# Two-layer expert model with a two-half second block: the memory's keys projected before each cross attention instead of in front of the experts

## The chip, the core and the metric

One core of a Trainium2 chip (trn2) runs the whole program. The metric is the device time of one execution in microseconds; the kernel before took 2755.97 us, the median of three runs.

The engines are TensorE (PE: matmuls and transposes; its weight loads, PEld, overlap them), VectorE (DVE), ScalarE (ACT), GpSimd (POOL) and SyncE (SP), which issues nearly all DMA transfers. Each engine runs its own queue strictly in order and waits on semaphores for the others.

## The reference, cut to what matters

512 tokens of width 1024, all float32. The first block has two layers of a mixer and 32 experts each. The second block has two halves: self attention, cross attention to a memory of 256 tokens, and a gated feed-forward, each with a norm before and a norm behind. Memory keys and values depend on nothing but the input `mem` and weights:

```python
def hier_moe(x, w_group, b_group, w_expert, b_expert, w1, w3, w2):
    ...
    def expert_block(args):
        rows, rw, e = args
        xi = x_pad[rows]
        h = jax.nn.silu(xi @ w1[e]) * (xi @ w3[e])
        return (h @ w2[e]) * rw[:, None]
    ...
def memory_cross_attention(u, mem_n, wq, wkv, wo):
    q = split_heads(u @ wq, X_HEADS)
    k, v = jnp.split(mem_n @ wkv, 2, axis=-1)
    k = split_heads(k, X_HEADS)
    v = split_heads(v, X_HEADS)
    s = jnp.einsum('bhqd,bhkd->bhqk', q, k,
                   preferred_element_type=jnp.float32) * (X_HEAD_DIM ** -0.5)
    p = jax.nn.softmax(s, axis=-1)
    o = jnp.einsum('bhqk,bhkd->bhqd', p.astype(v.dtype), v)
    return merge_heads(o) @ wo

    ...

        u = rms_norm_2(h, mem_pre_g[i])
        y = memory_cross_attention(u, rms_norm_2(mem, mem_kv_g[i]), x_wq[i], x_wkv[i], x_wo[i])
        h = h + rms_norm_2(y, mem_post_g[i])
```

## The kernel before

**Numbers.** A product of float32 matrices is made of three matmuls (`mm3`): each operand is split into a high part and a remainder (`wh`, `wl` for weights, `xth`, `xtl` for activations), and hi·hi, hi·lo and lo·hi are added in PSUM. ACT writes the high part, DVE the remainder (`split`, `wload`). For a projection the weights are loaded as tiles `raw` of [128, 1024], 512 KB, from a heap of 46 such tiles that all stages share. The experts' matmuls take the raw float32 tiles.

**Order.** The program writes its operations down in one order (`run`, L2299 on); a list scheduler (`flush`) then deals them to the engines. It keeps, per engine, a window of operations in the order in which they were written, and picks by a cost model (`price`, L215) when each is free and ready. The order that comes out is fixed: every engine runs its queue as written. All recorded instructions carry line L385.

**Stages.** Per layer of the first block: mixer (`f1`), router (`route`), then, before the change, `mem_kv(l)` (L1002) for half `l` of the second block, then the experts (`moe`). The router's DVE chain ends in slot lists (`slg`), permutation tiles (`P`) and token indices for GpSimd's gathers (`xg`), from which PE makes `xe`; each pair of experts then runs up (`mm<-raw,xe`), down (`mm<-raw,t`) and a combine. A loop for overflowing slots ahead of the experts is a barrier of all engines. Expert weights are `raw<-w` on SP's queue, 192 loads per layer.

`mem_kv(i)` loads the memory (two tiles `mem`), norms it (`xn<-mem`), transposes it (16 transposes, `tp<-const,xn`), projects the keys (8 chunks × 8 × 3 = 192 matmuls of 256 columns, `mm<-xth,wh 128x256` and its two fellows, out to `memk` in DRAM) and the values (96 matmuls of 512 columns, out to `memv`).

Each half of the second block is `longnet` or `diff` (self attention with its output projection), `cross` (L1033) and `ffn`. The tail of the output projection (`tail_post`, L722) works per tile of 128 tokens: adds the last partial sum (`y<-y,mm`), makes the norm's factor `n_r`, adds to `x` in two halves (`x<-y,n_r,x`, `x<-t,n_r,x`), and hands the tile to the chain (`chain`, L748), which transposes it (eight `tp<-const,x` per tile, 32 in all) and splits the result (`xtl<-tp,xth`). `cross` then projects q with `x_wq`: the first half of its columns in two token halves (192 matmuls of 256 columns), the rest in 96 of 512. It reads the keys back (`kraw`, split to `kh`, `kl`) and the values (`vraw`); its first score matmul is `mm<-kh,xth`.

```python
def to_T(s, t, xn, xT, pairs=None):
    ...
    for q in range(2) if pairs is None else ():
        tp = s.TP()
        for i in range(4):
            nc.tensor.transpose(tp[:, i * 128:(i + 1) * 128], ...)
```

Of the kernel before, what the change touches and what calls it, by code (L numbers as in the profile page):

```python
# [10 lines left out]
F32 = mybir.dt.float32  # L11
# [9 lines left out]
DSIZE = {F32: 4, F32R: 4, I32: 4, U32: 4, BF16: 2}  # L21
EPS = 1e-6
D = 1024
# [62 lines left out]
class Recorder:  # L86
# [127 lines left out]
    @staticmethod  # L214
    def price(eng, method, outs, ins, k):  # L215

        def free(x):
            n = 1
            for v in x.shape[1:]:
                n *= int(v)  # L220
            return n
        if eng == "ALL":
            return 2500, 0
        n = max(free(x) for x in outs + ins) if method != "matmul" else free(outs[0])
        if eng == "PE":
            dt = ins[-1].dtype if method == "matmul" else ins[0].dtype
            f = (2 if method == "transpose" else 4) if dt == F32 else 1
            if method == "matmul" and dt == F32 and outs[0].shape[0] == 64:

                f = 2  # L230
            return n * f * 0.417, None
        psum = any(x.tensor.space == PSUM for x in ins)
        if eng == "SP" or "dma" in method:
            b = outs[0] if outs[0].tensor.space != bass.MemoryType.DRAM else ins[0]
            return (1040, 4500 if "indirect" in method else 1710) if eng == "POOL" else (475, 1100), int(b.shape[0]) * free(b) * DSIZE[b.dtype] / 360
        small = sum(isinstance(x, bass.AP) for x in (k.get("scale"), k.get("bias"), k.get("accum_out")))
        if eng == "ACT":
            return (51 if psum else 93) + n * 0.833 + 93 * small, None
        if eng == "POOL":
            if k.get("op") == ALU.pow:  # L240
                return 300 + 165 * n, None
            return 150 + n * (1 if method == "memset" else 2.1), None
        fast = method in ("tensor_scalar", "tensor_copy", "memset") and not psum
        return 69 + n * (0.52 if fast else 1.04) + 61 * sum(free(x) == 1 for x in ins), None
# [230 lines left out]
class Kern:  # L475
# [102 lines left out]

    def wload(s, W, k0, nk, c0, ncol, gain=None, lo_eng="V"):

        nc = s.nc
        per = min(1024 // ncol, 4)
        res = []
        eng = lo_eng
        for a in range(0, nk, per):
            q = min(per, nk - a)
            raw, hi, lo = s.H(name="raw"), s.H(F32R, "wh"), s.H(F32R, "wl")
            nc.sync.dma_start(raw[:, :q * ncol].rearrange("p (j c) -> p j c", j=q),
                              W[(k0 + a) * 128:(k0 + a + q) * 128, c0:c0 + ncol].rearrange("(j p) c -> p j c", p=128))
            if gain is None:  # L590
                s.split(raw[:, :q * ncol], hi[:, :q * ncol], lo[:, :q * ncol])
            for i in range(q):
                v = slice(i * ncol, (i + 1) * ncol)
                if gain is not None:
                    s.split_gain(raw[:, v], hi[:, v], lo[:, v], gain[:, k0 + a + i:k0 + a + i + 1], eng[(a + i) % len(eng)])
                res.append((hi[:, v], lo[:, v]))
        return res
# [34 lines left out]

    def out_proj(s, actT, nk, W, resident, tail, k0=0, accum=None, post=None, gain=None):

# [4 lines left out]
        for a in range(0, nk, 4):  # L639
            m = min(4, nk - a)  # L640
            w = s.wload(W, k0 + a, m, 0, 512, gain)
            for t in range(NT):
# [23 lines left out]
        for a in range(0, nfree, 4):  # L666
            m = min(4, nfree - a)
            w = s.wload(W, k0 + a, m, 512, 512, gain)
            for t in range(NT):
                for i in range(m):  # L670
                    k = a + i
                    s.mm3(pss[t], actT.get(k, t * 128, t * 128 + 128), w[i],
                          k == 0, k == nk - 1)
        w = s.wload(W, k0 + nfree, resident, 512, 512, gain)
        for t in range(NT):
# [323 lines left out]
        return ys  # L999


    def mem_kv(s, i):  # L1002

        nc = s.nc
        W = s.I["x_wkv_2"][i]
        kd = s.dr.tile([D, 256], F32, name=f"memk{i}")
        vd = s.dr.tile([256, D], F32, name=f"memv{i}")
        g = s.gain(s.I["mem_kv_g_2"][i])
        mT = s.newXT(256)
        for t in range(2):  # L1010
            m = s.H(name="mem")
            nc.sync.dma_start(m, s.I["mem_2"][0, t * 128:(t + 1) * 128, :])
            xn = s.norm(m, g)
            s.to_T(t, xn, mT)
        for cb in range(2):
            def ck(c, ps):
                o = s.T2()
                nc.scalar.copy(o[:, 0:256], ps[:, 0:256])
                r = (cb * 4 + c) * 128
                nc.sync.dma_start(kd[r:r + 128, :], o[:, 0:256])  # L1020
            s.lin_T(mT, 8, W, cb * 512, 128, 4, ck)
        for cb in range(2):
            w = s.wload(W, 0, 8, D + cb * 512, 512)
            for t in range(2):
                ps = s.PS()
                for k in range(8):
                    s.mm3(ps, mT.get(k, t * 128, t * 128 + 128), w[k], k == 0, k == 7)
                o = s.T2()
                nc.scalar.copy(o, ps)
                nc.sync.dma_start(vd[t * 128:(t + 1) * 128, cb * 512:(cb + 1) * 512], o)  # L1030
        return kd, vd

    def cross(s, i, act, kv, nxt):  # L1033
        nc = s.nc
# [1266 lines left out]
    def run(s):  # L2301
        I = s.I
        s.setup()
        c = s.chain(I["attn_norm"][0])
        c.prep()
        for t in range(NT):
            c(t)
        kv = []
        for l in range(2):
            s.f1(l, c.act, s.chain_route(l), I["x"][0] if l == 0 else s.xd)  # L2310
            s.route()
            kv.append(s.mem_kv(l))
            raws = [s.pair_raw(l, p) for p in range(2)]
            c = s.chain(I["attn_norm"][1] if l == 0 else I["mix_pre_g_2"][0], s.spill)
            s.moe(l, raws, c)
        for i in range(2):
            n = s.chain(I["mem_pre_g_2"][i])
            (s.longnet, s.diff)[i](c.act, n, s.xd)
            c = s.chain(I["ffn_pre_g_2"][i])
            s.cross(i, n.act, kv[i], c)  # L2320
            n = s.chain(I["mix_pre_g_2"][1], s.spill) if i == 0 else s.store
            s.ffn(i, c.act, n)
            c = n
        s.nc.flush()
# [16 lines left out]
```

## Time and profile before

| | |
|---|---|
| median of 3 runs | 2755.97 us (2755.9 to 2762.24) |
| the profiled execution's own time | 2757.27 us |
| its span | 2755.5 us |
| mean granted clock of TensorE | 0.991 |
| PE busy | 2671.8 us, 97% |
| DVE, ACT, POOL busy | 1521.8, 1167.3, 637.5 us |
| DMA | 421.92 MB, mean 153 GB/s |

The profile is one execution seen by the hardware profiler. It was read in this order: the page's busy times; windows, which give busy time, granted clock (1.00 is 2.4 GHz) and DMA rate of a stretch; waits, which sum an engine's idle time by what ended it; and the timeline, which lists single instructions with their start, duration and the idle time before them. In the timeline `mm<-xth,wh 128*128 128x256` is a matmul with stationary `xth` and moving `wh` into a PSUM tile `mm` of 128 × 256. A matmul's duration includes the time until its result is there, so the price of one in a row of many is the distance between their starts.

### The profile page before, as it was taken

What the parts mean: (1) busy time and instruction counts of PE and PEld (TensorE: products, weight loads), DVE (VectorE), ACT (ScalarE), POOL (GpSimd) and SP (SyncE); (2) the same over time, 40 slices, a digit from 0 to 9 for tenths busy, and PEclk for the clock granted to TensorE, in tenths of its full rate; (3) what the DMA queues carried; (4) which work ended last, traced back from release to release, by engine and by line L of the source; (5) the groups of instructions that cost most, each with busy time, mean ns of one, the idle gap of its engine ahead of it and who ended that gap; (6) DMA issues with size and microseconds to landing.
All of it is one profiled execution on the core that took longest, in us unless ns stands there. A gap on an engine that the chain in (4) does not pass through costs nothing.

```text
span 2755.5 us, 40546 instructions
## 1 busy us (share of the span) xinstructions
PE 2671.8 (97%) x15112; PEld 2143.7 (78%) x15112; DVE 1521.8 (55%) x3259; ACT 1167.3 (42%) x2390; POOL 637.5 (23%) x754
## 2 busy tenths in 40 slices
PE   8999999999999999999999999999999999999998
PEld 7878765568888665568788988888888879888887
DVE  6696544355787443353698553344548885543433
ACT  5555212144455111154696452233447765432331
POOL 2623101004332100013364111001325541110012
PEclk9999999999999999999999999999999999999999
DMA  6125999961136999930113322333411133322321
GB/s 178 30 78 174 333 408 406 375 209 42 40 125 227 370 408 398 355 106 24 53 56 138 115 77 73 94 101 107 132 39 62 62 124 105 94 73 84 112 94 44
DMA packets 224056, 421.92 MB, mean 153 GB/s; under 512 B 46064, under 2 KB 112368, under 8 KB 223856
## 3 DMA queue, kind: packets, MB, share of 16 engines
q1 hardware_dynamic: 219248, 410.89, 42.7%
q0 software_dynamic: 4608, 8.40, 0.8%
q8 instruction: 121, 1.98, 0.3%
q14 instruction: 79, 0.65, 0.1%
HBM read 410.83 MB, written 16.78 MB: 155 GB/s over the span
## 4 chain that ended last, share of the span: by engine, by line
PE 58%; DVE 5%; ACT 2%; POOL 1%; issue 1%; DMA 0%; DVEq 0%; ACTq 0%; POOLq 0%
PE mm L385 54%; PE tp L385 3%; DVE wl L385 1%; DVE x L385 1%; DVE t L385 1%; ACT t L385 0%; DVE nm L385 0%; ACT qh L385 0%; DVE pt L385 0%; ACT pring L385 0%; POOL ra L385 0%; POOL t L385 0%; DVE y L385 0%; DMA raw<-x_wq 0%; DVE xnm L385 0%
## 5 line engine op out<-in xcount | busy, mean ns | idle before, releaser
L385 PE MATMUL mm<-wh,xth 128*128 128x512 f32 (+3 forms) x1088 | 404.9, 397 | 1.3 <-DVE xtl L385 0.7
L385 PE MATMUL mm<-wl,xth 128*128 128x512 f32 (+3 forms) x1088 | 402.9, 394 | 1.4 <-DVE wl L385 1.4
L385 PE MATMUL mm<-wh,xtl 128*128 128x512 f32 (+3 forms) x1088 | 402.2, 393 | 0.2 <-DVE xtl L385 0.2
L385 DVE SCALAR_TENSOR_TENSOR wl<-raw,pre_g,wh 128x512 fp32r<-128x512 f32 (+4 forms) x400 | 284.7, 752 | 150.2 <-ACT wh L385 120.2
L385 PE MATMUL mm<-xth,wh 128*128 128x512 f32 (+1 forms) x1184 | 365.6, 359 | 0.8 <-ACT xth L385 0.3
L385 PE MATMUL mm<-xth,wl 128*128 128x512 f32 (+1 forms) x1184 | 364.5, 358 | 0.0
L385 PE MATMUL mm<-xtl,wh 128*128 128x512 f32 (+1 forms) x1184 | 362.8, 357 | 1.5 <-DVE xtl L385 1.5
L385 ACT ACTIVATE wh<-raw,pre_g 128x512 fp32r<-128x512 f32 (+4 forms) x400 | 252.0, 686 | 68.8 <-DMA raw<-w_gate_up 49.1
L385 PEld LDWEIGHTS mm<-xtl,wh 128*128 128x128 f32 x1184 | 219.2, 190 | 32.8 <-DVE xtl L385 1.7
L385 PEld LDWEIGHTS mm<-xth,wh 128*128 128x128 f32 x1184 | 219.3, 190 | 32.3 <-ACT xth L385 0.8
L385 PEld LDWEIGHTS mm<-xth,wl 128*128 128x128 f32 x1184 | 219.4, 190 | 30.8
L385 PE MATMUL mm<-raw,xe 128*64 128x256 f32 x2048 | 234.3, 383 | 3.0 <-issue 3.0
L385 PEld LDWEIGHTS mm<-wh,xth 128*128 128x128 f32 x1088 | 204.9, 189 | 35.5 <-ACT xth L385 2.2
L385 PEld LDWEIGHTS mm<-wl,xth 128*128 128x128 f32 x1088 | 205.0, 189 | 35.2 <-DVE wl L385 2.3
L385 PEld LDWEIGHTS mm<-wh,xtl 128*128 128x128 f32 x1088 | 205.3, 189 | 33.1 <-DVE xtl L385 0.6
L385 PEld LDWEIGHTS mm<-raw,xe 128*64 128x64 f32 x2048 | 144.3, 137 | 85.1 <-issue 12.8
L385 POOL TENSOR_TENSOR ffl<-t,ffh 128x512 fp32r<-128x512 f32 x44 | 60.0, 1365 | 543.6 <-ACT ffh L385 505.7
L385 DVE TENSOR_TENSOR wl<-raw,wh 128x1024 fp32r<-128x1024 f32 x112 | 144.4, 1294 | 51.6 <-ACT wh L385 43.7
L385 ACT ACTIVATE t<-mm 128x256 f32<-128x256 f32 (+3 forms) x72 | 28.8, 403 | 290.3 <-PE mm L385 230.3
L385 ACT CAST wh<-raw 128x1024 fp32r<-128x1024 f32 (+2 forms) x128 | 120.1, 956 | 34.7 <-DMA raw<-w_down 29.7
L385 PE MATMUL mm<-raw,t 128*64 128x512 f32 x512 | 126.8, 641 | 7.5 <-ACT t L385 7.4
L385 PE MATMUL mm<-wh,ffh 128*128 128x512 f32 x352 | 130.1, 389 | 0.0
(338 smaller groups left out, 4911.3 us busy)
## 6 DMA issues: line engine op xcount, KB each, us to landing
raw<-w SPq DMA_DIRECT2D x384, 512.0 KB
raw<-w_gate_up SPq DMA_DIRECT2D x176, 256.0 KB
raw<-w_down SPq DMA_DIRECT2D x40, 512.0 KB
raw<-x_wkv SPq DMA_DIRECT2D x32, 512.0 KB
raw<-a_w_in SPq DMA_DIRECT2D x24, 512.0 KB
raw<-b_w_in SPq DMA_DIRECT2D x24, 512.0 KB
raw<-w_in SPq DMA_DIRECT2D x24, 384.0 KB
raw<-w_out SPq DMA_DIRECT2D x16, 512.0 KB
```

The lines of the kernel that those rows point to most:

```text
L385: r = o.fn(*o.a, **o.k)
```

## The change

`mem_kv` is cut in three. `mem_T` holds the norm and transposes of the memory, `mem_keys` is `mem_T` with the projection of the keys, `mem_values` is `mem_T` with that of the values. `mem_values` stays in front of the experts. `mem_keys` is called after the self attention of the half and before `cross`. Norm and transposes of the memory are thus done twice per half. `price` also reckons a DMA of long runs at 400 bytes per ns instead of 360, for the scheduler only.

```diff
@@ -230,9 +230,19 @@
                 f = 2
             return n * f * 0.417, None
         psum = any(x.tensor.space == PSUM for x in ins)
+
+        def s_rate(aps):
+
+            x = next(v for v in aps if v.tensor.space == bass.MemoryType.DRAM)
+            n = 1
+            for st, c in reversed(list(x.ap)):
+                if st != n and c > 1:
+                    break
+                n *= c
+            return 400 if n * 4 >= 4096 else 360
         if eng == "SP" or "dma" in method:
             b = outs[0] if outs[0].tensor.space != bass.MemoryType.DRAM else ins[0]
-            return (1040, 4500 if "indirect" in method else 1710) if eng == "POOL" else (475, 1100), int(b.shape[0]) * free(b) * DSIZE[b.dtype] / 360
+            return (1040, 4500 if "indirect" in method else 1710) if eng == "POOL" else (475, 1100), int(b.shape[0]) * free(b) * DSIZE[b.dtype] / s_rate(outs + ins)
         small = sum(isinstance(x, bass.AP) for x in (k.get("scale"), k.get("bias"), k.get("accum_out")))
         if eng == "ACT":
             return (51 if psum else 93) + n * 0.833 + 93 * small, None
@@ -999,26 +1009,36 @@
         return ys
 
 
-    def mem_kv(s, i):
-
-        nc = s.nc
-        W = s.I["x_wkv_2"][i]
-        kd = s.dr.tile([D, 256], F32, name=f"memk{i}")
-        vd = s.dr.tile([256, D], F32, name=f"memv{i}")
+    def mem_T(s, i):
+
         g = s.gain(s.I["mem_kv_g_2"][i])
         mT = s.newXT(256)
         for t in range(2):
             m = s.H(name="mem")
-            nc.sync.dma_start(m, s.I["mem_2"][0, t * 128:(t + 1) * 128, :])
+            s.nc.sync.dma_start(m, s.I["mem_2"][0, t * 128:(t + 1) * 128, :])
             xn = s.norm(m, g)
             s.to_T(t, xn, mT)
+        return mT
+
+    def mem_keys(s, i, kd):
+
+        nc = s.nc
+        W = s.I["x_wkv_2"][i]
+        mT = s.mem_T(i)
+        yield
         for cb in range(2):
             def ck(c, ps):
                 o = s.T2()
                 nc.scalar.copy(o[:, 0:256], ps[:, 0:256])
                 r = (cb * 4 + c) * 128
                 nc.sync.dma_start(kd[r:r + 128, :], o[:, 0:256])
-            s.lin_T(mT, 8, W, cb * 512, 128, 4, ck)
+            yield from s.lin_T_steps(mT, 8, W, cb * 512, 128, 4, ck)
+
+    def mem_values(s, i, vd):
+
+        nc = s.nc
+        W = s.I["x_wkv_2"][i]
+        mT = s.mem_T(i)
         for cb in range(2):
             w = s.wload(W, 0, 8, D + cb * 512, 512)
             for t in range(2):
@@ -1028,7 +1048,6 @@
                 o = s.T2()
                 nc.scalar.copy(o, ps)
                 nc.sync.dma_start(vd[t * 128:(t + 1) * 128, cb * 512:(cb + 1) * 512], o)
-        return kd, vd
 
     def cross(s, i, act, kv, nxt):
         nc = s.nc
@@ -2309,7 +2328,8 @@
         for l in range(2):
             s.f1(l, c.act, s.chain_route(l), I["x"][0] if l == 0 else s.xd)
             s.route()
-            kv.append(s.mem_kv(l))
+            kv.append((s.dr.tile([D, 256], F32, name=f"memk{l}"), s.dr.tile([256, D], F32, name=f"memv{l}")))
+            s.mem_values(l, kv[l][1])
             raws = [s.pair_raw(l, p) for p in range(2)]
             c = s.chain(I["attn_norm"][1] if l == 0 else I["mix_pre_g_2"][0], s.spill)
             s.moe(l, raws, c)
@@ -2317,6 +2337,7 @@
             n = s.chain(I["mem_pre_g_2"][i])
             (s.longnet, s.diff)[i](c.act, n, s.xd)
             c = s.chain(I["ffn_pre_g_2"][i])
+            s.merge(s.mem_keys(i, kv[i][0]))
             s.cross(i, n.act, kv[i], c)
             n = s.chain(I["mix_pre_g_2"][1], s.spill) if i == 0 else s.store
             s.ffn(i, c.act, n)
```

**PE at the first junction from self attention to cross attention.** `tp<-const,x` are the transposes of x, `mm<-wh,xth 128x512` and its fellows belong to the output projection of the self attention, `mm<-xth,wh 128x256` before the change to q; of before:

```order
L385 MATMUL tp<-const,x 128x128 x4
L385 MATMUL mm<-wh,xth 128x512
L385 MATMUL mm<-wl,xth 128x512
L385 MATMUL mm<-wh,xtl 128x512
L385 MATMUL mm<-xth,wh 128x256
L385 MATMUL mm<-xtl,wh 128x256
L385 MATMUL mm<-xth,wl 128x256
...
L385 MATMUL mm<-xth,wl 128x256
L385 MATMUL tp<-const,x 128x128 x4
L385 MATMUL mm<-xth,wh 128x256
L385 MATMUL mm<-xtl,wh 128x256
L385 MATMUL tp<-const,x 128x128 x4
```

and of the change, where `tp<-const,xn` are the transposes of the memory and the `128x256` matmuls are the keys:

```order
L395 MATMUL mm<-wh,xth 128x512
L395 MATMUL mm<-wl,xth 128x512
L395 MATMUL mm<-wh,xtl 128x512
L395 MATMUL tp<-const,x 128x128 x20
L395 MATMUL tp<-const,xn 128x128 x8
L395 MATMUL tp<-const,x 128x128 x4
L395 MATMUL tp<-const,xn 128x128 x8
L395 MATMUL mm<-xth,wh 128x256 x5
L395 MATMUL mm<-xtl,wh 128x256
L395 MATMUL mm<-xth,wl 128x256
L395 MATMUL mm<-xth,wh 128x256
```

The transposes of the last two tiles stood inside q; now those of all tiles but the first stand together with the memory's, ahead of the keys, and q stands behind the keys. The second half has the same pattern.

**DVE at the same junction**, of before, from the x of the last two tiles to the last split of the chain:

```order
L385 SCALAR_TENSOR_TENSOR x<-y,n_r,x 128x512
L385 SCALAR_TENSOR_TENSOR x<-t_3049,n_r,x 128x512
L385 SCALAR_TENSOR_TENSOR x<-y,n_r,x 128x512
L385 SCALAR_TENSOR_TENSOR x<-t_3057,n_r,x 128x512
L385 TENSOR_TENSOR vl<-vraw,vh 128x1024
L385 TENSOR_TENSOR xtl<-tp,xth 128x2x128 x7
L385 TENSOR_SCALAR pre_v<-nss 128x1 x2
L385 TENSOR_TENSOR xtl<-tp,xth 128x2x128
L385 TENSOR_TENSOR vl<-vraw,vh 128x1024
```

and of the change, where `xn<-mem` is the memory's norm and `wl<-raw,wh 128x1024` a split of the keys' weights:

```order
L395 TENSOR_TENSOR wl<-raw,wh 128x1024
L395 TENSOR_SCALAR n_r<-nss 128x1
L395 SCALAR_TENSOR_TENSOR x<-y,n_r,x 128x512
L395 TENSOR_TENSOR xtl<-tp,xth 128x2x128
L395 SCALAR_TENSOR_TENSOR xn<-mem,n_r,gain 128x1024
L395 TENSOR_SCALAR n_r<-nss 128x1
L395 TENSOR_TENSOR xtl<-tp,xth 128x2x128 x2
L395 SCALAR_TENSOR_TENSOR x<-t_2977,n_r,x 128x512
L395 SCALAR_TENSOR_TENSOR xn<-mem,n_r,gain 128x1024
L395 TENSOR_TENSOR xtl<-tp,xth 128x4x128
...
L395 TENSOR_SCALAR pre_v<-nss 128x1
L395 SCALAR_TENSOR_TENSOR wl<-raw,pre_g,wh 128x512 x8
```

The splits of q's weights (`wl<-raw,pre_g,wh`), which stood ahead of the chain, and those of keys and values (`kl`, `vl`) stand behind it now; the memory's norm and splits stand in it.

**SP in front of the first experts**, of before (`raw<-w` are expert weights):

```order
L385 DMA raw<-x_wkv 128x2x512 x6
L385 DMA xm_590<-xn 128x1024
L385 DMA raw<-x_wkv 128x2x512 x5
L385 DMA xm_590<-xn 128x1024
L385 DMA memk_665<-t_697 128x256
L385 DMA raw<-w 128x1024
L385 DMA pre_g<-attn_norm 128x8x1
L385 DMA raw<-w 128x1024 x3
L385 DMA memk_665<-t_699 128x256
L385 DMA raw<-w 128x1024 x9
L385 DMA memk_665<-t_701 128x256
```

and of the change:

```order
L395 DMA raw<-x_wkv 128x2x512 x3
L395 DMA xm_590<-xn 128x1024
L395 DMA raw<-x_wkv 128x2x512 x2
L395 DMA xm_590<-xn 128x1024
L395 DMA raw<-x_wkv 128x2x512 x3
L395 DMA raw<-w 128x1024
L395 DMA pre_g<-attn_norm 128x8x1
L395 DMA raw<-w 128x1024 x6
L395 DMA xm_590<-xn 128x1024
L395 DMA raw<-w 128x1024 x5
L395 DMA xm_590<-xn 128x1024
```

Eight loads of `x_wkv` and the stores of the keys no longer stand among and ahead of the expert weights.

## Rows read from the trace of the kernel before

**Rows 1.** The page: busy time of each engine, its share of the span, instructions.

```profile
PE 2671.8 (97%) x15112; PEld 2143.7 (78%) x15112; DVE 1521.8 (55%) x3259; ACT 1167.3 (42%) x2390; POOL 637.5 (23%) x754
```

**Rows 2.** Windows (start:end, length, busy us by engine, PE's granted clock, DMA share, GB/s): front, junction.

```profile
core 0: us, PE busy (x) PEld busy (x) DVE busy (x) ACT busy (x) POOL busy (x), PEclk, DMA share, GB/s
...
280.00:330.00 50.00, 50.00 (x383) 44.86 (x383) 33.26 (x138) 10.05 (x19) 7.42 (x7) 1.00 0.97 357
...
1490.00:1495.00 5.00, 4.88 (x17) 3.96 (x17) 3.15 (x9) 2.40 (x7) 0.55 (x1) 0.54 0.00 0
```

**Rows 3.** PE's waits, first expert stage (280 to 560): total us, times, longest.

```profile
PE tp L385 <- DVE t L385: 4.9, 4, 1.6
...
PE tp L385 <- DMA raw<-w: 1.4, 1, 1.4
```

**Rows 4.** Window 350 to 500; SP's waits from 340 to 400, and from 460 to 520.

```profile
350.00:500.00 150.00, 145.93 (x1014) 89.72 (x1014) 63.00 (x126) 26.39 (x49) 9.91 (x10) 1.00 1.03 407
...
SPq L385 <- DMA raw<-w: 41.3, 43, 2.4
...
SPq L385 <- PE mm L385: 31.2, 21, 4.6
```

**Rows 5.** Timeline of PE, first junction: start us, us, instruction [idle before <-releaser].

```profile
1488.61 1.08 PE L385 MATMUL tp<-const,x 128*128 128x128 f32 x4 [3.37 <-issue]
...
1496.85 0.27 PE L385 MATMUL mm<-xth,wh 128*128 128x256 f32 x1
...
1505.58 0.60 PE L385 MATMUL tp<-const,x 128*128 128x128 f32 x4
...
1542.28 0.28 PE L385 MATMUL mm<-kh,xth 128*128 128x256 f32 x1
```

**Rows 6.** Timeline of DVE, first junction.

```profile
1484.89 1.02 DVE L385 TENSOR_TENSOR n_r<-ss 128x1 f32<-128x1 f32 x1 [0.19 <-ACT t L385]
...
1486.77 1.74 DVE L385 SCALAR_TENSOR_TENSOR x<-y,n_r,x 128x512 f32<-128x512 f32 x1
...
1491.11 0.75 DVE L385 SCALAR_TENSOR_TENSOR x<-y,n_r,x 128x512 f32<-128x512 f32 x1 [0.67 <-POOL n_r L385]
...
1495.39 0.42 DVE L385 TENSOR_TENSOR xtl<-tp,xth 128x256 fp32r<-128x256 f32 x1 [1.54 <-ACT xth L385]
...
1502.30 0.75 DVE L385 SCALAR_TENSOR_TENSOR x<-y,n_r,x 128x512 f32<-128x512 f32 x1
```

**Rows 7.** Timelines of DVE (first line) and PE, second junction.

```profile
2252.26 1.24 DVE L385 TENSOR_TENSOR n_r<-ss 128x1 f32<-128x1 f32 x1
...
2261.99 0.74 PE L385 MATMUL mm<-xth,wh 128*128 128x256 f32 x4
...
2308.40 0.28 PE L385 MATMUL mm<-kh,xth 128*128 128x256 f32 x1
```

**Rows 8.** Timeline of PE, first front: keys, first expert matmul.

```profile
279.52 0.40 PE L385 MATMUL mm<-xtl,wh 128*128 128x256 f32 x2
...
279.99 0.40 PE L385 MATMUL mm<-xth,wh 128*128 128x256 f32 x2
...
328.42 3.67 PE L385 MATMUL mm<-raw,xe 128*64 128x256 f32 x32
```

**Rows 9.** Timeline of DVE, first routing chain.

```profile
282.90 1.21 DVE L385 TENSOR_TENSOR wl<-raw,wh 128x1024 fp32r<-128x1024 f32 x1
...
298.47 0.29 DVE L385 TENSOR_TENSOR t<-t,tp 128x128 f32<-128x128 f32 x1 [3.26 <-PE tp L385]
...
300.61 0.24 DVE L385 TENSOR_SCALAR slg<-rt_sl 128x8 f32<-128x8 f32 x2
...
310.64 3.71 DVE L385 TENSOR_SCALAR P<-const,slg 128x512 bf16<-128x512 f32 x8 [3.87 <-PE mm L385]
```

**Rows 10.** Timeline of SP's queue, first front: the first load of expert weights.

```profile
282.30 0.42 SPq L385 DMA_DIRECT2D raw<-w  x1
```

**Rows 11.** Timeline of DVE: norm of a memory tile.

```profile
261.93 1.27 DVE L385 SCALAR_TENSOR_TENSOR xn<-mem,n_r,gain 128x1024 f32<-128x1024 f32 x1
```

## Prediction

> **What bounds the kernel now.** I read the page first, then windows of the stages that the change touches, then the waits in them, and last single instructions. TensorE (PE) is busy for 2671.8 us [rows 1] of a span of 2755.5, so only some 84 us are not matmul work. The time is PE's work plus the few places where PE stands uncovered: moving a piece of PE work gains only if it covers more where it goes than where it was.
>
> The **front of the first experts** is PE's. PE is busy in all 50 us from 280 to 330 [rows 2], with the keys, the values and the routing sums. In the whole expert stage PE's largest wait is 4.9 us for a tile that DVE writes; it waits 1.4 us for expert weights [rows 3]. The DMA engines are full there (share 1.03, 407 GB/s), but SP, which issues the loads, waits first for earlier loads (41.3 of 60 us) and later for PE to free tiles (31.2 of 60) [rows 4]: loads run ahead, and PE sets the pace.
>
> The **junction** from the self attention to the cross attention is a chain on DVE: a tile's last norm, x, transposes, splits. In the first half PE stands 3.37 us before the first transposes at 1488.61, then runs the projection's left-over matmuls, and takes up the q projection at 1496.85 [rows 5], while x of the last tiles is only made at 1502.30 [rows 6] and their last transposes stand inside q, at 1505.58 [rows 5]. So q covers the second part of the chain. In the second half the chain begins at 2252.26 and q at 2261.99 [rows 7].
>
> **The change part by part.** *Keys leave the front.* Per half 192 matmuls of 256 columns go. Four of them take 0.47 us (279.52 to 279.99) [rows 8], so 0.12 each and 23.0 us. By PE alone the first expert matmul would come at 328.42 − 23.0 = 305.4. It also needs the routing chain: slg at 300.61, P at 310.64 for 3.71 us [rows 9], then sums, gather and transposes until 328.42, 14.1 us after P. Eight weight splits wl (spacing 1.15) leave that chain, 9.2 us, a wait of 3.26 us for a transpose on PE shrinks by an unknown part [rows 9], and P now follows slg at once. So slg comes at 291.4 with that wait or 288.1 without, P ends 3.7 later, and the first expert matmul stands at 309.2 or 305.9. The front gains 19 to 22.5 us; I take 21, between its two ends, and the same for the second layer, which is built alike: −42.
>
> Eight of the 16 loads of x_wkv also leave SP's queue, 512 KB each. A load takes about 1.3 us in the full stretch (512 KB at 407 GB/s [rows 4]), so expert weights begin some 10 to 16 us before 282.30 [rows 10], where PE wants them 21 earlier. The lead of the loads over PE is 328.42 − 282.30 = 46 us today and would be 35 to 41. With 1.4 us of waits on loads today I cost that at nothing; if the lead were too short, it is the third rival. The barrier of the overflow loop moves ahead of the first expert matmul; every engine pays it once either way, nothing. The planner's new DMA rate leaves the order elsewhere nearly as it was: nothing.
>
> *Keys come to the junction*, +23.0 us of PE per half. In PE's new order all 32 transposes of x and all 16 of the memory stand ahead of the first key matmul, and q behind the keys. So keys start only when the DVE chain ends, and q covers none of it. DVE's work, in the new order from the first n_r to the memory's second xn: n_r 1.0; three tail sums, 1.8; eight halves of x, two at 1.7 (beside GpSimd) and six at 0.67; three wl, 3.4; two xn, 2.4; pairs and singles of xtl (0.34 each), about 4; small ones, 0.9 [rows 6, 9, 11]. That is 20.9 us, and the last eight transposes with ACT's cast behind it 1.5. DVE's waits in this stretch are now 0.67 and 1.54 [rows 6] and shorter ones, 2.6 in all. So keys start 25 us after the first n_r. The ends are 20 (norms of the memory slip into DVE's waits) and 28 (tail sums wait behind the ten left-over matmuls at the lower clock).
>
> Then come keys, 23.0, and q. From 1496.85 to the first score matmul (kh) at 1542.28 are 45.4 us; less some 1.4 for the 16 transposes inside, q takes 44.0 [rows 5]. The first score matmul now comes 25 + 23.0 + 44.0 = 92.0 us after the first n_r, where today it is 1542.28 − 1484.89 = 57.4 [rows 5, 6] and 2308.40 − 2252.26 = 56.1 [rows 7]: +34.6 and +35.9. Of these 70.5 us, 46.0 are the keys and 24.5 is the lost cover of q, the repeated norm of the memory and its transposes within it.
>
> *Loads at the junction.* Two memory tiles, a gain and 8 x_wkv loads are added; SP passes them ahead of x_wq, half of which now waits for tiles that the keys free. The DMA share in this stretch is 0.00 [rows 2], and 23 us of keys lie over it: nothing; without that cover four loads, 5 us.
>
> *Clock.* After the wait of 3.37 us the granted clock reads 0.54 from 1490 to 1495 [rows 2, 5], about 1.2 GHz, so those 5 us lose 2.3. The new wait is longer and broken by transposes; the first keys may run at the lower level too, 0 to 3 us per half. I take nothing, since the loss of today is in the 57.4, and keep 3 for the range. The Trainium skill ("TensorE: Matmul & The Clock Gate", section "What's actually happening") says that the throttled state is the default and activity releases it. By that rule, which speaks against the change, both halves begin their keys at 1.2 GHz and the sum would be some 5 us higher; the first junction's row agrees with the rule.
>
> **Sum:** −42 + 70.5 = +28.5 us. The profiled execution took 2757.27 us, 1.3 above the median of 2755.97, so 2785.8 in its terms and 2784.5 in those of the median. I predict **2784 us**, 1% slower. A measurement of this kernel can tell 0.3%, 8.3 us, from no change.
>
> **The rivals.** *First, faster: keys before x.* The keys need nothing of x. If PE began them at the first n_r, they would fill the 3.37 us, the chain would run under them, and q would follow whole: 23.0 + 15 left-over matmuls (3.4) + 48 transposes (4.5) + 44.0 = 75 us, +17.5 and +18.8. With −42 that is −6; with the front at its best (−23 each) −10, so 2746 to 2750. For it: memory and its weights can lie ready early. Against it: PE's new queue, with 48 transposes ahead. It decides for faster only if keys start within a few us of the first n_r. Chance 0.08.
>
> *Second, no change: a short chain.* q's 15 splits no longer lie ahead of the chain, nor kl and vl in it (four operations like wl, 4.6 us). If keys start after 14 us, the junctions cost 23.6 + 24.9 = 48.5, the sum is +6.5 and the time 2762. For it: some of the chain is waiting, which another order may fill. Against it: wl, xn and the memory's xtl take the place of what goes. Chance 0.14.
>
> *Third, much slower: loads set the experts' pace.* Then a half gains in front only its 8 loads, 10.4 us, and the sum is 70.5 − 20.8 = +50: 2806. For it: DMA share 1.03. Against it: PE's 1.4 us. Chance 0.10. [...]
>
> **How the numbers follow.** The forecast has 0.68. Its own range, with the chain at 20 to 28 us, the clock and the front's ends, is 2771 to 2798. The range to hold 8 in 10 is **2758 to 2802**: it takes in the second rival and leaves out the first and the third. Faster 0.09, same 0.13, slower 0.78.
>
> **What would show it.** Right: no keys in the first front and its expert matmuls 19 to 22.5 us earlier; at both junctions PE idle for some 10 to 13 us more, among transposes, first key matmul 20 to 28 us after the first n_r, then 23 us of keys and 44 of q; PE's busy time up by a few us. Wrong: keys among the projection's left-over matmuls; a front that hardly moves; or PE waiting for expert weights far longer than 1.4 us.

## The result and the profile after

The changed kernel takes **2781.55 us** (median of four runs, 2779.26 to 2787.06) against 2757.41 for the kernel before in the same comparison: ratio 1.0083, 95% interval 1.007 to 1.0097. That is 24.1 us slower, where 28.5 were forecast (2784 us, range 2758 to 2802). The profiled execution took 2787.06 us with a span of 2785.3, at the upper end of the runs, so its stages sum to some 6 us more than the medians differ.

The page's line of busy times, which answers to [rows 1]:

```profile
PE 2687.9 (97%) x15144; PEld 2163.5 (78%) x15144; DVE 1523.7 (55%) x3275; ACT 1176.6 (42%) x2406; POOL 642.4 (23%) x758
```

PE's busy time grew by 16 us for 32 more transposes (some 4 us). Eight transposes are busy for 1.97 us at a granted clock of 0.50 and for 1.08 us as it comes back (both below), so a stretch of lower clock shows in the busy time too.

To see where the time went, I cut the timeline of PE at the same instructions in each trace: the first transposes of x that feed the router, the first and the last up matmul of a layer's experts (start to start), the first transposes of x at a junction, the first score matmul. Times between them in us:

| stretch | before | change | move alone | rate alone | rate 440 | move, 440 |
|---|---|---|---|---|---|---|
| start to first layer's router | 245.1 | 254.2 | 247.2 | 255.1 | 245.9 | 246.6 |
| router to first expert matmul, layer 1 | 83.3 | 70.2 | 71.4 | 85.8 | 89.8 | 74.4 |
| first to last expert up matmul, layer 1 | 262.7 | 250.1 | 264.0 | 250.9 | 236.7 | 237.8 |
| router to first expert matmul, layer 2 | 86.1 | 68.5 | 67.4 | 85.2 | 87.7 | 71.8 |
| first to last expert up matmul, layer 2 | 260.1 | 249.9 | 261.5 | 250.0 | 237.8 | 235.8 |
| first junction, to the first score matmul | 53.7 | 87.9 | 87.4 | 53.2 | 53.1 | 87.5 |
| second junction | 52.1 | 88.0 | 88.0 | 52.1 | 52.2 | 87.9 |
| all the rest | 1712.4 | 1716.5 | 1711.4 | 1711.7 | 1709.4 | 1707.5 |

The last four columns are experiments, below. The up matmuls of the first layer, before and with the change, as the view of the tile `xe` lists them (durations in ns, then the first and the last start):

```profile
L385 PE MATMUL mm<-raw,xe x1024: 379/379/687, 328.4 to 591.1; 128*64 128x256 f32 x171
L395 PE MATMUL mm<-raw,xe x1024: 379/379/687, 324.4 to 574.5; 128*64 128x256 f32 x171
```

From before to the change, the junctions cost 34.2 + 35.9 = 70.1 us, the fronts give back 13.1 + 17.6 = 30.7, the expert stages give back 12.6 + 10.2 = 22.8, and the first layer's mixer takes 9.1 more: +25.7, with the rest +29.8. Of the rest's 4.1 us, 3.7 are in the second layer's mixer (240.8 for 237.1 us, at a mean granted clock of 0.97 for 0.99). The forecast had the junctions right, and missed the others with errors that nearly cancel.

The expectations recorded below give smaller values for the expert stages (256.2 and 253.4 us before, 244.2 and 243.7 with the rate alone, 247.7 and 241.1 with the rate for expert weights only). Those end at the start of a row that merges many matmuls, up to 7 us ahead of the last one; a range given for a stage there is best read as a difference from these values.

**The junction.** PE's timeline of the change, first junction, start us, us, instruction [idle before <-releaser], answers to [rows 5]:

```profile
1454.62 1.32 PE L395 MATMUL tp<-const,x 128*128 128x128 f32 x8 [1.09 <-DVE x L395]
1460.42 1.97 PE L395 MATMUL tp<-const,x 128*128 128x128 f32 x8 [4.49 <-DVE x L395]
1464.18 1.12 PE L395 MATMUL tp<-const,x 128*128 128x128 f32 x4 [1.79 <-DVE x L395]
1465.80 1.94 PE L395 MATMUL tp<-const,xn 128*128 128x128 f32 x8 [0.50 <-DVE n_r L395]
1467.53 1.04 PE L395 MATMUL tp<-const,x 128*128 128x128 f32 x4
1468.39 1.08 PE L395 MATMUL tp<-const,xn 128*128 128x128 f32 x8
1470.51 1.11 PE L395 MATMUL mm<-xth,wh 128*128 128x256 f32 x5 [1.05 <-ACT xth L395]
...
1537.61 0.28 PE L395 MATMUL mm<-kh,xth 128*128 128x256 f32 x1
```

Each of the waits shown before transposes of x ends with x on DVE. Nothing lies between the waits but transposes, and the keys start at 1470.51. DVE in the same stretch, answering to [rows 6]:

```profile
1444.43 0.38 DVE L395 TENSOR_TENSOR n_r<-ss 128x1 f32<-128x1 f32 x1 [0.85 <-ACT t L395]
...
1464.38 1.27 DVE L395 SCALAR_TENSOR_TENSOR xn<-mem,n_r,gain 128x1024 f32<-128x1024 f32 x1
...
1466.96 1.27 DVE L395 SCALAR_TENSOR_TENSOR xn<-mem,n_r,gain 128x1024 f32<-128x1024 f32 x1
```

From the first n_r at 1444.43 to the first key are 26.1 us, and to the first score matmul 93.2; the forecast had 25 and 92.0. In the second half (first line DVE, the others PE), answering to [rows 7], they are 25.0 and 92.1:

```profile
2246.23 0.52 DVE L395 TENSOR_TENSOR n_r<-ss 128x1 f32<-128x1 f32 x1 [0.87 <-ACT t L395]
...
2271.21 1.11 PE L395 MATMUL mm<-xth,wh 128*128 128x256 f32 x5 [0.35 <-ACT xth L395]
...
2338.30 0.28 PE L395 MATMUL mm<-kh,xth 128*128 128x256 f32 x1
```

The windows of the first junction, columns as in [rows 2]:

```profile
1455.00:1460.00 5.00, 0.93 (x7) 0.45 (x5) 5.00 (x13) 4.47 (x12) 3.27 (x3) 0.82 0.35 121
1460.00:1465.00 5.00, 2.79 (x12) 2.29 (x12) 4.11 (x10) 4.09 (x10) 2.62 (x3) 0.50 0.00 0
1465.00:1470.00 5.00, 3.96 (x22) 3.29 (x20) 5.00 (x10) 5.00 (x12) 0.55 (x1) 0.66 0.00 0
1470.00:1475.00 5.00, 4.49 (x35) 4.30 (x36) 5.00 (x12) 2.72 (x6) 1.54 (x2) 1.00 0.01 3
```

DVE is busy almost throughout, PE is not. The granted clock is 0.50 (1.2 GHz) while PE waits and transposes, and 1.00 from the first keys on, so the transposes paid for the lower clock and the keys did not.

**The front of the experts.** Windows of the change, columns as in [rows 2]:

```profile
280.00:310.00 30.00, 30.00 (x190) 24.47 (x188) 27.19 (x132) 6.43 (x13) 8.99 (x7) 1.00 1.03 408
310.00:330.00 20.00, 9.99 (x80) 6.75 (x78) 4.30 (x15) 1.17 (x2) 2.22 (x2) 0.66 0.79 270
```

PE is full until 310 and then half idle. Its waits from 260 to 560 (total, times, longest us), answering to [rows 3]:

```profile
PE tp L395 <- issue: 10.0, 1, 10.0
PE tp L395 <- DVE t L395: 3.0, 2, 1.5
PE mm L395 <- ACT t L395: 1.4, 3, 0.5
```

One wait of 10.0 us stands at the barrier of the overflow loop. The kernel before waits 3.0 us there, at 338.00, behind its first expert matmuls; that row belongs to the list of [rows 3], where it is the longest single wait. In the second layer the barrier takes 8.2 us against 2.0. The rows, before in the first layer, then the change and before in the second:

```profile
PE mm L385 <- issue: 3.0, 1, 3.0
...
PE tp L395 <- issue: 8.2, 1, 8.2
...
PE tp L385 <- issue: 2.0, 1, 2.0
```

Behind the barrier PE's clock is down, and the first expert matmuls take 5.59 us where they took 3.67 [rows 8] (first line DVE, then PE):

```profile
298.66 3.26 DVE L395 TENSOR_SCALAR P<-const,slg 128x512 bf16<-128x512 f32 x8
...
320.51 0.19 PE L395 MATMUL tp<-rt_rec,P 128*128 128x6 bf16 x1 [9.99 <-issue]
...
324.45 5.59 PE L395 MATMUL mm<-raw,xe 128*64 128x256 f32 x32
```

P stands 44.4 us behind the router's first transposes (298.66 and 254.24), where it stood 65.6 behind them in [rows 9]: 21 us earlier, as forecast. But from P's end to the first expert matmul 22.5 us pass, where the forecast kept the 14.1 of before. That stretch holds the barrier, and there the front loses 8.4 us of its gain. No wait on expert weights is left among PE's waits: the loads were early enough, with their first issue at 271.72 instead of 282.30 [rows 10].

### The profile page after: what moved, and what is told of

Its sections match the earlier page's. It is cut to its first block, busy times and chain, and to the rows that moved or that the text cites. A ratio compares the mean times of both kernels' runs of the same rounds, so it can differ in the third digit from the quotient of the medians.

```text
span 2785.3 us, 40687 instructions
## 1 busy us (share of the span) xinstructions
PE 2687.9 (97%) x15144; PEld 2163.5 (78%) x15144; DVE 1523.7 (55%) x3275; ACT 1176.6 (42%) x2406; POOL 642.4 (23%) x758
## 4 chain that ended last, share of the span: by engine, by line
PE 82%; DVE 9%; ACT 3%; POOL 2%; issue 2%; DMA 1%; SPq 0%; DVEq 0%; ACTq 0%; POOLq 0%
PE mm L395 75%; PE tp L395 7%; DVE wl L395 2%; DVE t L395 2%; DVE x L395 1%; DMA raw<-w 1%; ACT t L395 1%; DVE qkm L395 1%; POOL t L395 1%; ACT wh L395 0%; ACT qh L395 0%; SPq L395 0%; DVE nm L395 0%; DVE pt L395 0%; POOL ra L395 0%
## 5 line engine op out<-in xcount | busy, mean ns | idle before, releaser
L395 ACT ACTIVATE wh<-raw,pre_g 128x512 fp32r<-128x512 f32 (+4 forms) x400 | 252.7, 686 | 70.2 <-DMA raw<-w_gate_up 48.7
L395 PEld LDWEIGHTS mm<-xtl,wh 128*128 128x128 f32 x1184 | 219.1, 189 | 30.7
L395 ACT CAST wh<-raw 128x1024 fp32r<-128x1024 f32 (+1 forms) x128 | 120.8, 955 | 37.0 <-DMA raw<-w_down 30.2
L395 ACT ACTIVATE t<-mm 128x256 f32<-128x256 f32 (+3 forms) x72 | 28.7, 402 | 243.9 <-PE mm L395 153.6
L395 PE MATMUL mm<-wh,ffl 128*128 128x512 f32 x352 | 129.1, 390 | 0.0
```

The lines of the kernel that those rows point to most:

```text
L395: r = o.fn(*o.a, **o.k)
```

## The experiments

All kernels are compared with the kernel before in the same job; its medians there were 2756.5 to 2758.9 us. Diffs are against the kernel before or the change, as said.

### The planner's rate alone

The kernel before with the new `s_rate` in `price` and nothing else.

```diff
-            return (...) if eng == "POOL" else (475, 1100), ... / 360
+            return (...) if eng == "POOL" else (475, 1100), ... / s_rate(outs + ins)
```

> The kernel before with only the planner's new DMA rate (400 instead of 360 for long runs); keys stay in front of the experts. Theory A (the rate reorders the mixer of the first layer, where the profile of the change shows TensorE's granted clock at 0.50 to 0.85 in stretches that stood at 1.00, and route transposes 9.2 us later): 4 to 10 us slower than before, 2761 to 2767, with the same low clock between 120 and 195 us. Theory B (the low clock there is chance of one run): within 3 us of before, 2755 to 2760.

Measured: 2751.56 us, ratio 0.9974 (0.996 to 0.9988). Both theories are wrong about the total. The mixer is 10.0 us longer, as theory A said, but the expert stages are 11.8 and 10.1 us shorter. The windows of the mixer (110 to 245), of the kernel before and then of this one, columns as in [rows 2]:

```profile
110.00:245.00 135.00, 131.37 (x786) 109.12 (x785) 108.77 (x281) 67.25 (x169) 42.21 (x51) 1.00 0.27 85
```

```profile
110.00:245.00 135.00, 131.74 (x750) 110.20 (x749) 106.66 (x280) 65.13 (x167) 40.58 (x50) 0.92 0.27 84
```

PE is as busy, at a granted clock of 0.92, and gets through less work. So "the planner's new DMA rate: nothing" was wrong, twice and in both directions.

### The move alone

The change with `return 360` in `s_rate`.

> The change without the planner's new rate (360 everywhere). Theory A: the junctions lose as they did (first score matmul 87.9 us after the first transposes of x, +34 to +36 each), the mixer of the first layer runs as in the kernel before, so 4 to 10 us less than the change: 2772 to 2778, still slower than before. Theory B (the rate does nothing): the time of the change, 2779 to 2784.

Measured: 2801.97 us, ratio 1.0153 (1.0129 to 1.0178), 20 us more than the change. The mixer is at 247.2 us and the junctions at 87.4 and 88.0, as theory A said. The total is 24 us beyond theory A all the same, since without the rate the expert stages are back at 264.0 and 261.5. The move by itself costs about 44 us, and the rate hides nearly half of it.

### Keys and values apart, both in front

The move alone, with the keys called ahead of `mem_values`:

```diff
+            s.merge(s.mem_keys(l, kv[l][0]))
             s.mem_values(l, kv[l][1])
...
-            s.merge(s.mem_keys(i, kv[i][0]))
```

> mem_keys and mem_values both in front of the experts, each with its own norm and transposes of the memory, old rate: the price of doing the memory's norm twice, with no move. Theory A (only 16 transposes more per half, 1.9 us on TensorE, and a norm that hides): 2 to 6 us slower than before, 2758 to 2763. Rival (the second norm lengthens the routing chain in front of the experts, which sets the first expert matmul): 10 us or more slower, over 2767.

Measured: 2772.67 us, ratio 1.005 (1.0034 to 1.0066), the rival's size but not its place. The fronts take 84.6 and 83.2 us (83.3 and 86.1 before); the loss lies in the second layer's expert stage, 272.6 instead of 260.1, 7.6 us of it in waits at "issue". The price of the second norm could not be read from this run, since the planner ordered other work anew.

### Keys behind q

The move alone, with the keys written behind the q projection:

```diff
             s.lin_T(xT, 8, s.I["x_wq_2"][i], cb * 512, 128, 4, cq, halves=cb == 0, gain=act.g)
+        s.merge(s.mem_keys(i, kd))
...
-            s.merge(s.mem_keys(i, kv[i][0]))
```

> Keys between the self attention and the scores as in the change, but written behind the q projection, old rate; the memory's transposes then stand inside q, and q covers the chain of x again. Theory A (the loss at the junction is the lost cover of q, 11 to 13 us per half, and the keys' own 23 us): first score matmul 77 to 80 us after the first transposes of x, instead of 87.9; the whole 20 to 26 us under the move alone: 2750 to 2757. Rival (the loss is the repeated norm and the loads, wherever the keys stand): no more than 5 us under the move alone, 2770 or more.

Measured: 2796.83 us, ratio 1.0135 (1.0111 to 1.0159), only 5 us under the move alone, so theory A's total is missed by 40 us. At the junctions theory A holds: the first score matmul comes after 80.0 and 77.0 us instead of 87.4 and 88.0, with the norm and the transposes of the memory still there. But from there to the next stage it takes 68.3 and 69.7 us where all other kernels take 64.0. So of the 18.3 us that q's cover gave, the scores gave back 10.0: in the first half's scores PE waits 2.5 us for GpSimd's `pring`, where the kernel before waits 0.3. The expert stages are those of the move alone; the self attention of the first half takes 2.9 us more, with a wait of 3.2 us at "issue" before the first transposes of x. Why was not tried.

### Keys with their input from DRAM

The change, with the transposed memory stored once in front and read back:

```diff
-        mT = s.mem_T(i)
+        mT = s.newXT(256)
+        for q in range(2):
+            raw = s.H(name="mraw")
+            nc.sync.dma_start(raw, s.mT[i][q * 128:(q + 1) * 128, :])
+            s.split(raw, mT.h[q], mT.l[q])
...
     def mem_values(s, i, vd):
...
+        for q in range(2):
+            o = s.H(name="mo")
+            nc.vector.tensor_add(o, mT.h[q], mT.l[q])
+            nc.sync.dma_start(s.mT[i][q * 128:(q + 1) * 128, :], o)
...
+        s.mT = [s.dr.tile([256, D], F32, name=f"memT{i}") for i in range(2)]
```

> The change, rate included, but the memory is normed and transposed once, in front; its transposed form goes out to DRAM and is read back for the keys (two loads and two splits instead of norm and 16 transposes). The keys' matmuls then stand among the transposes of x, as q's did before. Theory A (the change loses q's cover, 11 to 13 us per half, because the keys wait for the memory's transposes): first score matmul 74 to 79 us after the first transposes of x instead of 87.9, whole 20 to 26 us under the change: 2755 to 2762. Rival (the junction is long for its loads and splits): 85 us or more, whole 2775 or more.

Measured: 2764.93 us, ratio 1.0027 (1.0017 to 1.0038), 17 us under the change and 3 over theory A; the first score matmul after 73.9 and 73.3 us. PE's timeline, first junction:

```profile
1463.01 0.27 PE L395 MATMUL mm<-xth,wh 128*128 128x256 f32 x1
...
1465.99 0.60 PE L395 MATMUL tp<-const,x 128*128 128x128 f32 x4
```

The keys begin 5.4 us after the first transposes of x (1457.58), and later transposes of x stand among them, as they stood among q. The junction is 14.0 and 14.6 us shorter than in the change, and 20.2 and 21.2 us longer than before, a little less than the keys' 23.0. So with the keys among the transposes of x the cover is back: it was the order of PE's queue that lost it. This kernel also has no norm and no transposes of the memory at the junction, so its 28.7 us are cover and norm together. With the cover back it is still no faster than before: the junctions cost 41.4 us and the fronts give back 26.6.

### No overflow loop

Two kernels without `s.overflow(l)`, the change and the rate alone; neither computes tokens over an expert's capacity.

> The change without the overflow loop, the barrier of all engines in front of the experts (tokens over an expert's capacity would not be computed). With the change TensorE waits 10.0 and 8.2 us at that barrier, where the kernel before waits 3.0 and 2.0. Theory D (the front gains less than the keys' 23 us because the barrier waits for the gathers, which the keys used to cover): from the router's first transposes to the first expert matmul 58 to 65 us instead of 70.2 and 68.5; the whole 12 to 20 us under the change. Rival (the gathers themselves set the first expert matmul, barrier or not): at most 4 us shorter per layer.

> The kernel before with the rate of the change, without the overflow loop (tokens over an expert's capacity would not be computed): what the barrier costs while the keys still stand in front. Theory D: the front shrinks by no more than 5 us per layer from 85.8 and 85.2, so that the change in the front comes nearer to the keys' 23 us once the barrier is gone. Rival: it shrinks as much as with the keys gone.

Measured: 2773.89 us (ratio 1.0062, 1.0045 to 1.0078) and 2745.69 us (0.9954, 0.9937 to 0.9971). The fronts are 64.6 and 62.7 us with the keys gone, 83.7 and 85.7 with the keys there. Without the barrier, taking the keys away gains 19.1 + 23.0 = 42.1 us, the forecast's 42; with it, 15.6 + 16.7 = 32.3 (the change against the rate alone). Theory D holds for the front: the keys had covered the barrier. The change's total fell by 8 us only by the medians, not by 12 to 20, and by 15.6 by the spans of the two profiles (2785.3 and 2769.7); the second expert stage came out at 254.3 instead of 249.9. So the total does not tell the theories apart.

### The rate for expert weights only, at 400, and with the move

Against the rate alone, and against the change:

```diff
-            return 400 if n * 4 >= 4096 else 360
+            return 400 if n * 4 >= 4096 and len(x.tensor.shape) == 4 else 360
```

> The kernel before with the planner's rate of 400 for the expert weights only; all other transfers stay at 360. The rate alone made the expert stages 12 and 10 us shorter (first to last expert matmul 256.2 and 253.4 us before, 244.2 and 243.7 with it) and the first layer's mixer 10 us longer (first transposes of the router at 245.1 and 255.1). Theory C (two separate effects of the planner, the first through the experts' order, the second through other transfers): expert stages 243 to 247, router at 245 to 249, whole 2732 to 2744. Rival (the longer mixer and the shorter experts hang together, or either is chance): 2750 or more.

> The change with the planner's rate of 400 for the expert weights only. Theory C: expert stages 243 to 248 us as in the change, router at 246 to 251 us instead of 254.2, junctions as in the change (87 to 89 us): 2772 to 2780. Rival (the rate of the other transfers is what the moved keys need): 2785 or more.

Measured with the keys in front: 2746.12 us, ratio 0.9956 (0.9943 to 0.9969). The expert stages are 254.4 and 247.8, 8.3 and 12.3 us shorter than before, but the router is at 250.7, halfway: the rate of the expert weights alone lengthens the mixer too, so theory C's two separate effects are not shown. The total lies between both guesses, 2 us over theory C's. With the move: 2788.12 us (2774.61 to 2795.09), ratio 1.01 (1.0075 to 1.0125), expert stages 253.7 and 255.9, some 4 and 6 us longer than in the change, router 249.3, junctions 87.9 and 88.0. Router and junctions are theory C's, the stages are not, the total is beyond the rival's bound, and its runs spread over 20 us, so this run decides nothing.

### The rate at 440 and at 500

As above, with 440 and with 500 for expert weights, keys in front.

> The kernel before with the planner's rate for the expert weights at 440 instead of 360, above the 407 that the trace shows. In TensorE's order of the first expert stage a pair's down matmuls stand straight behind the transposes that feed them 8 times before, 6 times at 400 and twice at 440; elsewhere other matmuls stand between. Theory E (the rate gains because such places cost about 3.7 us each: 1.5 of waiting for DVE, 0.46 for ACT and 1.7 of matmuls at the lower clock): expert stages 228 to 240 us instead of 247.7 and 241.1, whole 2722 to 2740. Rival (the loads, at 407 GB/s, cannot follow such an order): TensorE waits for expert weights, stages of 245 or more, whole 2748 or more.

> The kernel before with the planner's rate for the expert weights at 500. TensorE's order of the expert stages is that of 440 except at the end. Theory E: no further gain, 2712 to 2721. Rival (the planner issues loads in an order that the chip cannot follow): over 2725, with TensorE waiting for expert weights.

Measured at 440: **2716.51 us**, ratio 0.9845 (0.9825 to 0.9866), faster than both kernels and 6 us under theory E's range. The expert stages are 236.7 and 237.8, 26.0 and 22.3 us shorter than before, while the fronts ahead of them are 6.5 and 1.6 us longer. PE's waits in the second expert stage, of the kernel before, with the window from its first expert matmul to the next stage behind (columns as in [rows 2]):

```profile
PE tp L385 <- DVE t L385: 7.9, 7, 1.5
PE mm L385 <- ACT t L385: 3.7, 8, 0.5
...
924.50:1195.50 271.00, 259.40 (x1751) 154.45 (x1751) 99.95 (x189) 46.50 (x88) 16.78 (x21) 0.97 0.92 358
```

and the same at 440:

```profile
PE mm L395 <- ACT t L395: 1.4, 2, 0.7
...
907.70:1157.80 250.10, 248.70 (x1768) 155.43 (x1768) 111.15 (x209) 51.56 (x96) 16.76 (x21) 1.00 0.98 384
```

The waits for DVE are gone, PE is busy for 248.70 of 250.10 us at full clock, and the loads keep up at 384 GB/s. Two such places of the kernel before show what they cost:

```profile
454.55 0.48 PE L385 MATMUL tp<-const,t 128*128 128x128 f32 x2 [1.51 <-DVE t L385]
455.49 3.65 PE L385 MATMUL mm<-raw,t 128*64 128x512 f32 x16 [0.46 <-ACT t L385]
...
523.70 0.48 PE L385 MATMUL tp<-const,t 128*128 128x128 f32 x2 [1.56 <-DVE t L385]
524.64 5.35 PE L385 MATMUL mm<-raw,t 128*64 128x512 f32 x16 [0.46 <-ACT t L385]
```

Behind nearly the same waits sixteen down matmuls take 3.65 us at the first place and 5.35 at the second, where the granted clock is 0.68 from 524.6 to 530. The kernel before has 8 such places per layer, and at 6 of the 16 the matmuls take 5.3 us or more; so theory E's 3.7 us is the price of the dearest places, and the others cost their waits alone, 0.5 to 2.0 us. Together they cost 13.5 and 16.8 us per layer before, and 1.4 at 440, where 2 places are left. From the router's first transposes to the next stage a layer is 18.3 and 19.3 us shorter at 440 (356.2 and 357.1 us before), so these places are most of the gain; what the rest is was not traced. At 440 the planner puts other work, mostly the next pair's up matmuls, between such operations.

At 500: 2750.71 us, ratio 0.9969 (0.9956 to 0.9982), stages 252.7 and 253.6. The rival was right that it is slower, but PE does not wait for expert weights. Timelines of DVE, then PE, then PE in the second stage:

```profile
572.15 0.22 DVE L395 TENSOR_TENSOR par<-par 128x64 f32<-128x64 f32 x1 [21.12 <-DMA par<-a_k_head_norm]
```

```profile
574.41 0.67 PE L395 MATMUL tp<-const,t 128*128 128x128 f32 x2 [12.53 <-DVE t L395]
...
1165.79 6.55 PE L395 MATMUL mm<-raw,t 128*64 128x512 f32 x16 [14.72 <-ACT t L395]
```

DVE stands 21.12 us at an operation of the next layer's parameters, whose small load SP issues only at 568.09, behind its last expert loads; the expert tile t that PE needs is behind it on DVE. In the second stage ACT stands 19.60 us at a split of the next stage's weights, and PE 14.72 for a tile behind it. So here the order puts operations whose loads are not there yet ahead of tiles that PE needs.

### The move with the rate at 440

The kernel of the move with 400 for expert weights, at 440.

> The change with the planner's rate for the expert weights at 440, to set beside the kernel before with the same rate (2716.5 us, expert stages 234.1 and 231.9): in both, TensorE's order of the expert stages is now nearly the same, so the difference is the price of the move by itself. Theory F (the planner's side effects aside, the move costs the junctions 34 to 36 us each and gives back 14 to 18 us per front): expert stages 231 to 238, whole 36 to 46 us over the other, 2752 to 2762. Rival (with the loads this far ahead the front gives back the keys' whole 23 us per half): 20 to 28 us over, 2737 to 2745.

Measured: 2759.0 us, ratio 1.0003 (0.9989 to 1.0017), 42 us over the same without the move (40 us when each is set against the kernel before in its own job, 37 by the spans of the two profiles, 2749.5 and 2712.5). The expert stages differ by no more than 2.0 us now, so this is the price of the move: junctions +34.4 and +35.7, fronts −15.4 and −15.9. Theory F holds.

## Why the prediction was right, and where its steps failed

**Keys come to the junction: right, to a us.** Keys were to start 25 us after the first n_r and the first score matmul at 92.0; measured 26.1 and 25.0, 93.2 and 92.1. For cover, norm and transposes together 24.5 us had been put down. The kernel with the input from DRAM, whose keys stand among the transposes of x and which has no second norm there, is 28.7 us shorter at the junctions, loads and all. The kernel with the keys behind q keeps norm, transposes and loads, and is 18.3 us shorter there than the move alone. So most of it is q's lost cover; how much of the rest is the norm is not shown. One sign of the prediction did not come: PE's idle time from the first n_r to the first score matmul grew by 7.0 us (3.5 to 10.5) and 5.8 us (2.9 to 8.7), not by 10 to 13. The rest of the loss is in busy time, in more transposes and at the lower clock.

**Clock: the choice of nothing was right for the keys.** They ran at full clock. The Trainium skill ("TensorE: Matmul & The Clock Gate", section "What's actually happening") has the throttled state as the default that activity releases. The windows agree, 0.50 among the scattered transposes and 1.00 in the keys; but the release came in time, so the 5 us that the rule would have added at the keys did not come.

**Keys leave the front: the term was mis-sized.** Forecast −42, measured −30.7. The routing chain did shrink: P came 21 us earlier behind the router, within the 19 to 22.5. The step that failed is the barrier, "every engine pays it once either way, nothing", and with it the 14.1 us from P to the first expert matmul, taken as fixed: they became 22.5. The keys and the first expert matmuls had been its cover: its wait grew from 3.0 and 2.0 us to 10.0 and 8.2. Without the barrier the term is 42.1 us.

**The planner's rate: the step that failed most.** It was costed at nothing since few rows moved elsewhere. By itself it shortened the expert stages by 21.9 us and lengthened the mixer by 10.0; with the move these are 22.8 and 9.1. In the expert stages it is mostly a matter of a few places in PE's queue, where down matmuls stand right behind the transposes they need: 8 per layer before, 6 with the rate alone, 5 in the change, 2 at 440. The errors, +11.3 in the fronts, −22.8 in the expert stages, +9.1 in the mixer and +4.1 in the rest, with −0.4 at the junctions, sum to +1.3. So the junctions were foreseen, and that the total was met as well is luck.

**The rivals.** Keys before x: the order of PE's queue ruled it out, and the kernel that comes nearest to it gained 17 us over the change. A short chain: no, 25 and 26 us. Loads that set the pace: no. The Trainium skill ("Perfetto Trace Analysis", section "What 'DMA-bound' means") lists the DMA engines among the things that a DMA-bound kernel is bound on. They are busy all through the stage here (share 1.03 [rows 4]), but they did not set its length: at 440, with the same loads, it is 21 us shorter (250.10 for 271.00), PE busy for 248.70 us of it.

What stays open: why the mixer's order under the full rate has the lower clock; what inside the barrier takes its 8 to 10 us; and why runs of one kernel spread by 10 to 20 us in several of these comparisons.

## What to carry to other kernels

Before moving a piece of matmul work, ask what it covers where it stands (here routing, gathers and a barrier) and whether its inputs are there early enough to cover anything where it goes; matmuls that wait for the same engine as their neighbours cover nothing. A constant in a scheduler's cost model is a change to the whole program: try it by itself, and compare stage by stage, since a total can be right by errors that cancel. Short producer-consumer distances on an in-order engine (transposes, then the matmuls that read them) are worth counting in the emitted order.

## What the runs showed that was not expected

The order of the expert stages, with the same instructions and bytes, is worth 22 to 26 us per stage: 262.7 and 260.1 us at a planned rate of 360, 236.7 and 237.8 at 440, 252.7 and 253.6 at 500, though the trace's own rate is 407 GB/s [rows 4]. Waits of 1.56 and 0.46 us on PE are at some places followed by matmuls that take 5.35 instead of 3.65 us, and then cost nearly twice what the list of waits shows; at most places they cost no more than it shows.
